# A hybrid encoder block: q and k of the second half of the heads are turned by VectorE and through memory instead of by TensorE, and some scalings and casts go to ScalarE

## The chip, the cores and the metric

The kernel runs on one core of one Trainium2 chip. The metric is the device time of one execution in microseconds; of several executions the median counts. Five engines work side by side: PE (TensorE, the matmuls), DVE (VectorE), ACT (ScalarE), POOL (GpSimd) and SP (SyncE, which only starts transfers). Each carries out its own list of instructions in a fixed order and waits on semaphores for the others. PEld is the loading of PE's stationary operand.

## The reference

One layer of an encoder over 512 tokens of width 1024 in float32:

```python
x = x + 0.5 * swiglu_1(rmsnorm(x))
h = rmsnorm(x)
xr, gr, q, k, v, ga, gb = split(h @ w_in)
xc = centred_dwconv(xr)                                   # width 4
y_lru = (rglru_forward(xc) + rglru_backward(xc)) * gelu(gr)
q = rmsnorm_per_head(q) * q_norm * 64 ** -0.5             # 16 heads of 64
k = rmsnorm_per_head(k) * k_norm
y_att = neighbourhood_attention(q, k, v, rel_pos_bias)    # grid of 8 rows x 64 columns, window 8 x 16
y = sigmoid(ga) * y_lru + sigmoid(gb) * y_att
x = x + y @ w_out
x = x + 0.5 * swiglu_2(rmsnorm(x))
```

## The kernel before, in words

All operands stay in SBUF as tiles of 128 partitions; feature-major tiles hold 128 features by 512 tokens. A float32 product is made of three matmuls: both factors are split into a high part (h) in a reduced format and the rest (l), and h·h, h·l and l·h are added in PSUM. For a weight, `load_w` fetches 128x1024 numbers as `wraw` on SP's queue, ScalarE writes `wh` (L138, or VectorE's cast L140 where `act` is false) and VectorE writes `wl` as the difference (L141). There are four buffers of `wh` and of `wl`, so the split of a chunk's weights waits for the last matmul of the chunk four before it. `feat_chunk` makes one output tile from eight such pieces: 24 matmuls of 128x512 (L165 to L167).

The program is, in order: the first FFN; the projections `wxr` with the convolution; six groups `wqkv` that make q, k and v token-major, for the two halves of the heads (hf 0 and 1, eight heads each); the merge gates (`gates`, 24 chunks of `wg3`: first the gelu gate of the recurrent branch, w = 0, then the two sigmoid gates as tanh); `wout`; the second FFN. Beside them run "lanes", Python generators that `weave` advances by the rates of `RATE` after each chunk or half chunk: the recurrence ("lru"), V through memory ("v"), and the attention ("att" and "tail").

The attention lane of a half is `heads`. It first scales q and k by the root mean square per head (L983). Then it goes through four tiles, fi = 0 to 3, of two heads each. `start(fi)` turns the token-major q and k into feature-major ones: eight transposes on PE into two PSUM tiles (L992, L994), from which ScalarE writes `qh` and `kh` (L998, L1001) and VectorE `ql` and `kl` (L1000, L1003), with the norm's gains `gq8` and `gk` multiplied in. The tile's scores are 24 matmuls (L1024; in the second half together, in the first twelve and twelve), the first of which reads `kl`. VectorE adds the bias and takes the maximum (L1044), ScalarE the exp with its sum (L1051), VectorE the reciprocal (L1053) and the product with 1/sum (L1056). `ship` turns the probabilities with VectorE's 32x32 transposes (L1065, L1066), stores them to memory (`pd`, SP's queue, L1068) and fetches them back regrouped (`PT`, four transfers on GpSimd's queue, L1072). `apply` multiplies them with V on PE (L1087) and ScalarE takes the result out of PSUM (`att`, L1097).

A merge gate's chunk ends in VectorE's product with 1/rms (L1150, `pair`), which also frees the PSUM tile; ScalarE applies gelu or tanh to two chunks at once (L1154), and VectorE multiplies by the branch (`A`, L1164, L1167, L1173, L1174).

The final order of each engine's list is made by a scheduler from the order in the program, priorities and its own estimate of times. `tc.high_priority()` moves an instruction forward, `after(a, b)` puts it behind another, and `hold` puts it behind the matmul that was emitted last. The kernel's own table `RATE` and these marks are thus what decides where the attention's steps stand among the chunks. `big_t` hands out one of 42 equal buffers (`NBIG`), `pair_t` one of four double ones.

Of the kernel before, what the change touches and what calls it, by code (L numbers as in the profile page):

```python
# [77 lines left out]
RATE = {  # L78
    "xr": {"att": 0.0, "lru": 2.75},
    "t0": {"att": 0.0, "lru": 3.25},  # L80
    "t1": {"att": 0.75, "tail": 0.75, "lru": 2},
    "g": {"att": 0.7, "tail": 0.7, "lru": 1.5, "v": 0.5},
}


# [1 line left out]
def block_kernel(ctx: ExitStack, tc, a, out):  # L87
# [156 lines left out]
    def hold(i):  # L244

        after(i, mark["mm"])
        return i
# [389 lines left out]
        end(t1, o)  # L637


    lanes = {"att": [], "tail": [], "lru": [], "v": []}  # L640
    due = {"att": 0.0, "tail": 0.0, "lru": 0.0, "v": 0.0}

    def weave(rate):
        for ln, n in rate.items():
# [138 lines left out]
    def lru():  # L783
# [52 lines left out]
        def use(f, d):  # L836
            r, ix = got[f, d]
            hold(nc.vector.tensor_tensor(ix, ix, xc[f], ALU.mult))
            th = big_t(n="th")
# [72 lines left out]
    def qk_raw(w, hf, st):  # L912
        raws = []
        for ps in tok_group(w, hf):
            t = big_t(n="qk")
            with tc.high_priority():
                copy = nc.scalar.activation(t, ps, AF.Copy)
            raws.append(t)
        for j, t in enumerate(raws):
            sq = big_t(n="sq")  # L920
# [46 lines left out]
            if g == 0:  # L967
                after(ld, mark["xr"])

    def heads(hf, raws, st):  # L970

        rq = tiny.tile([P, 2, NCB, 8], F32, tag="rq", name=nm("rq"))
        for w in range(2):
# [3 lines left out]
        hold(nc.scalar.activation(rq, rq, AF.Sqrt))  # L977
        nc.vector.reciprocal(rq, rq)
        yield
        for w in range(2):  # L980
            for j in range(NCB):
                t = raws[w][j].rearrange("p (h d) -> p h d", d=HD)
                hold(nc.vector.tensor_tensor(t, t, rq[:, w, j, :].unsqueeze(2).to_broadcast([P, 8, HD]), ALU.mult))  # L983
            yield
        qk, rss, soft, PTs = {}, {}, {}, {}


        def start(fi):
            fs = slice(fi * P, (fi + 1) * P)
            pq, pk = aux_t(), aux_t()  # L990
            for j in range(NCB):
                hold(nc.tensor.transpose(pq[:, j * P : (j + 1) * P], raws[0][j][:, fs], ident))  # L992
            for j in range(NCB):
                hold(nc.tensor.transpose(perm(pk)[:, j], raws[1][j][:, fs], ident))  # L994
# [3 lines left out]
            nc.scalar.activation(rev(qh), fwd(pq), AF.Copy, scale=gq8)  # L998
            with tc.high_priority():
                nc.vector.scalar_tensor_tensor(rev(ql), fwd(pq), gq8, rev(qh.bitcast(F32)), ALU.mult, ALU.subtract)  # L1000
            nc.scalar.activation(kh, pk, AF.Copy, scale=gk)  # L1001
            with tc.high_priority():
                mark["kl"] = nc.vector.scalar_tensor_tensor(kl, pk, gk, kh.bitcast(F32), ALU.mult, ALU.subtract)  # L1003
            grid = lambda t: t.rearrange("p (r c) -> p r c", r=ROWS)
            qk[fi] = qh, ql, grid(kh), grid(kl)

        def scores(fi, n2s):
# [22 lines left out]
            for n2, hp in [(n2, hp) for n2 in n2s for hp in range(2)]:  # L1030
# [22 lines left out]
                nc.vector.reciprocal(rs[:, hp, n2 * 2 : n2 * 2 + 2], rs[:, hp, n2 * 2 : n2 * 2 + 2])  # L1053
                for i, pt in enumerate(parts):
                    n = n2 * 2 + i
                    nc.vector.tensor_scalar(pt, pt, rs[:, hp, n : n + 1], None, ALU.mult)  # L1056
# [79 lines left out]
    for hf in range(2):  # L1136
        st = tiny.tile([P, 2, NCB, 8], F32, tag="st", name=nm("st"))
        raws = [qk_raw(0, hf, st), qk_raw(1, hf, st)]
        v_get(hf)
        lanes["att"].append(heads(hf, raws, st))  # L1140
        phase[0] = "t1" if hf == 0 else "g"


    def gates(w, fs, fn, scale=1.0):
        q = [pair_t() for _ in range((len(fs) + 1) // 2)]
        for i, f in enumerate(fs):
            ps = acc_t()
            feat_chunk(a["wg3"][w * KT + f], KT, xh, xl, ps, 0, KT, f % 2 == 0, RATE[phase[0]])
            with tc.high_priority():
                nc.vector.tensor_tensor(q[i // 2][:, i % 2], ps, rb, ALU.mult)  # L1150
            weave(RATE[phase[0]])
        for i, t in enumerate(q):
            n = min(2, len(fs) - 2 * i)
            nc.scalar.activation(t[:, :n], t[:, :n], fn, scale=scale)  # L1154
        return [(f, q[i // 2][:, i % 2]) for i, f in enumerate(fs)]
# [133 lines left out]
```

## Time and profile before

| | |
|---|---|
| median of 3 executions | 1088.83 us (1087.8 to 1089.4) |
| the profiled execution | 1086.2 us |
| its span, first to last instruction | 1084.4 us |
| matmuls of the span | 5121 |
| instructions of VectorE, ScalarE, GpSimd | 1222, 866, 340 |
| HBM read and written | 162.06 MB, 26.74 MB |

Rows of the profile read: start and length in us, engine, line of the kernel, operation, tiles written and read, shapes, count, and in brackets the idle time of that engine before it with the instruction that ended it. Rows of groups carry the number of instructions, their busy time and the mean of one in ns, then the idle time ahead of them. Rows of the chain of work that ended last carry start, length and group. In rows of DMA issues the last number is the median time from issue to landing. PE's matmuls overlap, so their durations in a timeline are longer than the time from one to the next.

### The profile page before, as it was taken

How to read it: one execution, taken by the hardware profiler on the slowest of the kernel's cores; microseconds unless marked ns; L12 is line 12 of the kernel's file. 1: busy time of each engine (PE TensorE's matmuls, PEld its weight loads, DVE VectorE, ACT ScalarE, POOL GpSimd, SP SyncE). 2: the span in 40 equal slices, each digit the busy share in tenths (PEclk: the TensorE clock that was granted, in tenths of full speed). 3: DMA queues.
4: the chain of work that ended last, by engine and by line, in shares of the span. 5: the costliest groups of instructions: out<-in, count | busy, mean ns of one | idle time of the engine just before them, and what ended most of it. 6: DMA issues, size and time to landing. Idle time of an engine off the chain costs nothing.

```text
span 1084.4 us, 14405 instructions
## 1 busy us (share of the span) xinstructions
PE 1076.1 (99%) x5121; PEld 883.1 (81%) x5121; DVE 770.8 (71%) x1222; ACT 562.1 (52%) x866; POOL 199.6 (18%) x340
## 2 busy tenths in 40 slices
PE   9999999999999999999999999999999999999998
PEld 7878888888888778788887888888888888888887
DVE  7798788774327876999868996759677787765322
ACT  7755554553215768877454642346455555544320
POOL 0101012432000441330345232000000001342000
PEclk9999999999999999999999999999999999999999
DMA  9878675975324675573787567564476777676222
GB/s 356 183 231 224 192 174 143 242 257 156 98 83 146 183 239 156 164 215 95 226 245 222 175 215 231 164 233 162 95 193 181 192 205 165 179 249 195 95 73 78
DMA packets 67464, 198.18 MB, mean 183 GB/s; under 512 B 11072, under 2 KB 12864, under 8 KB 67392
## 3 DMA queue, kind: packets, MB, share of 16 engines
q1 hardware_dynamic: 46736, 136.66, 37.6%
q0 software_dynamic: 20512, 60.34, 24.9%
q8 instruction: 40, 0.66, 0.3%
q14 instruction: 32, 0.26, 0.1%
q10 hardware_dynamic: 144, 0.26, 0.1%
HBM read 162.06 MB, written 26.74 MB: 174 GB/s over the span
## 4 chain that ended last, share of the span: by engine, by line
PE 95%; DVE 3%; issue 1%; DMA 1%; ACT 1%; SPq 0%; DVEq 0%; ACTq 0%
PE acc L315 19%; PE aux L315 14%; PE acc L165 10%; PE acc L166 10%; PE acc L167 10%; PE acc L905 4%; PE acc L906 4%; PE acc L907 4%; PE aux L166 4%; PE aux L167 4%; PE aux L165 4%; PE aux L1087 1%; PE aux L816 1%; PE aux L1024 1%; DVE wl L141 1%; PE aux L472 1%
## 5 line engine op out<-in xcount | busy, mean ns | idle before, releaser
L141 DVE TENSOR_TENSOR wl<-wraw,wh 128x1024 fp32r<-128x1024 f32 (+2 forms) x147 | 168.9, 1150 | 152.4 <-ACT wh L138 151.9
L138 ACT ACTIVATE wh<-wraw 128x1024 fp32r<-128x1024 f32 (+2 forms) x135 | 134.7, 999 | 214.9 <-PE acc L166 155.5
L141 DVE TENSOR_TENSOR wl<-pair,wh 128x1024 fp32r<-128x1024 f32 x80 | 97.5, 1222 | 43.7 <-ACT wh L138 43.5
L138 ACT ACTIVATE wh<-pair 128x1024 fp32r<-128x1024 f32 x80 | 84.7, 1062 | 77.5 <-PE aux L315 48.3
L165 PE MATMUL acc<-xh,wh 128*128 128x512 f32 x288 | 113.9, 396 | 0.0
L167 PE MATMUL acc<-xh,wl 128*128 128x512 f32 x288 | 112.5, 391 | 0.0
L166 PE MATMUL acc<-xl,wh 128*128 128x512 f32 x288 | 112.5, 391 | 0.0
L315 PE MATMUL aux<-wh,s 128*128 128x512 f32 x320 | 98.4, 389 | 0.2 <-ACT wh L138 0.2
L315 PE MATMUL acc<-wh,s 128*128 128x512 f32 x320 | 98.5, 389 | 0.0
L905 PE MATMUL acc<-wh,xh 128*128 128x512 f32 x192 | 75.7, 394 | 0.0
L906 PE MATMUL acc<-wh,xl 128*128 128x512 f32 x192 | 74.8, 389 | 0.0
L907 PE MATMUL acc<-wl,xh 128*128 128x512 f32 x192 | 74.7, 389 | 0.0
L315 PEld LDWEIGHTS aux<-wh,s 128*128 128x128 f32 x320 | 60.0, 188 | 13.0 <-ACT wh L138 0.6
L315 PEld LDWEIGHTS acc<-wh,s 128*128 128x128 f32 x320 | 60.1, 188 | 12.4
L166 PE MATMUL aux<-hl,wh 128*128 128x512 f32 (+1 forms) x179 | 69.3, 387 | 0.0
L167 PE MATMUL aux<-hh,wl 128*128 128x512 f32 (+1 forms) x179 | 69.3, 387 | 0.0
L165 PE MATMUL aux<-hh,wh 128*128 128x512 f32 (+1 forms) x179 | 69.0, 387 | 0.0
L167 PE MATMUL acc<-hh,wl 128*128 128x512 f32 (+1 forms) x176 | 68.1, 387 | 0.0
L166 PE MATMUL acc<-hl,wh 128*128 128x512 f32 (+1 forms) x176 | 68.1, 387 | 0.0
L165 PE MATMUL acc<-hh,wh 128*128 128x512 f32 (+1 forms) x176 | 68.0, 387 | 0.0
L165 PEld LDWEIGHTS acc<-xh,wh 128*128 128x128 f32 x288 | 54.1, 188 | 13.0 <-issue 2.3
L167 PEld LDWEIGHTS acc<-xh,wl 128*128 128x128 f32 x288 | 54.1, 188 | 11.5 <-issue 0.4
(230 smaller groups left out, 2416.5 us busy)
## 6 DMA issues: line engine op xcount, KB each, us to landing
wraw<-wqkv SPq DMA_DIRECT2D x24, 512.0 KB, 4.5
wraw<-wg SPq DMA_DIRECT2D x24, 512.0 KB, 7.5
wraw<-w1d SPq DMA_DIRECT2D x22, 512.0 KB, 4.2
wraw<-w2d SPq DMA_DIRECT2D x22, 512.0 KB, 3.3
PT<-w1s SPq DMA_DIRECT2D x20, 512.0 KB, 6.2
hT<-hd POOLq DMA_DIRECT2D x80, 128.0 KB, 4.2
PT<-w2s SPq DMA_DIRECT2D x20, 512.0 KB, 3.9
hd<-ht SPq DMA_DIRECT2D x32, 256.0 KB, 5.9
```

The source lines that it names most:

```text
L138: mark["H"] = nc.scalar.activation(H, raw, AF.Copy)
L141: return nc.vector.tensor_tensor(L, raw, H.bitcast(F32), ALU.subtract)
L165: nc.tensor.matmul(ps, wh, xh, start=first, stop=False, skip_group_check=skip)
L166: nc.tensor.matmul(ps, wh, xl, start=False, stop=False, skip_group_check=skip)
L167: mark["mm"] = nc.tensor.matmul(ps, wl, xh, start=False, stop=last, skip_group_check=skip)
L315: mark["mm"] = nc.tensor.matmul(pss[tb], x_[:, s], w_[:, c], start=first and k == 0 and x_ is xh_ and w_ is H, stop=k == 3 and w_ is L, sk ...
L472: nc.tensor.matmul(pre[tb], xh[k][:, s], H, start=k == 0, stop=False)
L816: prev, mm = mm, nc.tensor.matmul(ps[d][b], W[w][o, c], X[x][o], start=x == 1, stop=w + x == 0)
L905: nc.tensor.matmul(pss[j], xh[kk][:, tj], H[:, s], start=kk == 0, stop=False)
L906: nc.tensor.matmul(pss[j], xl[kk][:, tj], H[:, s], start=False, stop=False)
L907: mark["mm"] = nc.tensor.matmul(pss[j], xh[kk][:, tj], L[:, s], start=False, stop=kk == KT - 1)
L1024: mm = hold(nc.tensor.matmul(ps[hp][:, cs], q_[o, n * P : (n + 1) * P], keys(k_[o]), start=k_ is kl, stop=q_ is ql))
```

## The change

For the second half, hf = 1, `heads` is cut in two. A new lane, "prep", runs `norm_qk`: it scales q and k as before, turns each 128 tokens of them by 32x32 blocks on VectorE (L991), stores the four results (512 KB each) to memory as `qd` on SP's queue, and then fetches tile 0. `fetch(fi)` brings one tile's q and k back regrouped by four transfers on GpSimd's queue (L1010; each 32 partitions by 16 runs of 64 numbers) into the one buffer `xqk`; that of fi + 1 is emitted at the end of `start(fi)`. `start` of the second half has no transposes and reads `xqk` instead of PSUM. The gain of k is multiplied into that of q, so that `kh` and `kl` are a plain copy and difference; the copies to `qh` and `kh` are now held behind the matmul emitted last. The first half keeps its transposes (now L1027, L1029).

Besides, the products with 1/sum go from VectorE to ScalarE in both halves (L1098), and all casts of the merge gates' weights go to ScalarE, where before every second one was VectorE's. To make room, `NBIG` is 40, squares use the `pt` buffers and three `th` tiles those of `xqk` and `PT`. The multiply that ends a gate chunk is L1197 in the new file, `ql` and `kl` are L1040 and L1043, the maxima L1086, the score matmuls L1066, the A products L1211, `pt`'s transposes L1107 and L1108.

```diff
 RATE = {
...
-    "t1": {"att": 0.75, "tail": 0.75, "lru": 2},
-    "g": {"att": 0.7, "tail": 0.7, "lru": 1.5, "v": 0.5},
+    "t1": {"att": 0.75, "tail": 0.75, "lru": 2, "prep": 1.0},
+    "g": {"att": 0.7, "tail": 0.7, "lru": 1.5, "v": 0.5, "prep": 1.0},
...
-    NBIG = 42
+    NBIG = 40
...
-    gk = small[:, C_KN : C_KN + 1]
+    nc.vector.tensor_tensor(gq8, gq8, small[:, C_KN : C_KN + 1], ALU.mult)
...
-    def heads(hf, raws, st):
+    def norm_qk(raws, st, qd):
...
+        out = []
+        for j in range(NCB):
+            for w in range(2):
                 t = raws[w][j].rearrange("p (h d) -> p h d", d=HD)
                 hold(nc.vector.tensor_tensor(t, t, rq[:, w, j, :].unsqueeze(2).to_broadcast([P, 8, HD]), ALU.mult))
+            if qd is not None:
+                t2 = pair_t().rearrange("p a b -> p (a b)")
+                for w in range(2):
+                    nc.vector.transpose(
+                        t2.rearrange("p (c f w i) -> p w f c i", c=NCB, f=4, w=2)[:, w],
+                        raws[w][j].rearrange("p (f c i) -> p f c i", c=NCB, i=32))
+                while out:
+                    hold(nc.sync.dma_start(*out.pop()))
+                out.append((qd[j], t2))
+                yield
+            elif j % 2 == 1:
+                yield
+        if qd is not None:
+            hold(nc.sync.dma_start(*out.pop()))
             yield
+            fetch(qd, 0)
+
+    xs = {}
+
+    def fetch(qd, fi):
+        t = xs[fi] = big.tile([P, NCB * NCB, 2, 32], F32, tag="xqk", bufs=1, name=nm("xqk"))
+        for c in range(NCB):
+            hold(nc.gpsimd.dma_start(
+                t[c * 32 : (c + 1) * 32].rearrange("p g w i -> p g (w i)"),
+                qd.rearrange("j (a i) c f x -> c f i (j a) x", a=NCB)[c, fi]))
+
+    def heads(hf, raws, qd):
+
+        if hf == 1:
+            until("prep", lambda: False)
...
         def start(fi):
...
+            else:
+                x = xs.pop(fi).rearrange("p (j a) w i -> p w j a i", j=NCB)
+                xq, xk = x[:, 0], x[:, 1].rearrange("p j a (r c) -> p j a r c", r=2)
+                q_of = lambda t: rev(t).rearrange("p j (a i) -> p j a i", i=32)
+                k_of = lambda t: t.rearrange("p (a r j c) -> p j a r c", a=NCB, r=2, j=NCB)
             qh, ql, kh, kl = (big_t(F32R, n=n) for n in ("qh", "ql", "kh", "kl"))
-            nc.scalar.activation(rev(qh), fwd(pq), AF.Copy, scale=gq8)
+            hold(nc.scalar.activation(q_of(qh), xq, AF.Copy, scale=gq8))
...
-            nc.scalar.activation(kh, pk, AF.Copy, scale=gk)
+            hold(nc.scalar.activation(k_of(kh), xk, AF.Copy))
             with tc.high_priority():
-                mark["kl"] = nc.vector.scalar_tensor_tensor(kl, pk, gk, kh.bitcast(F32), ALU.mult, ALU.subtract)
+                mark["kl"] = nc.vector.tensor_tensor(k_of(kl), xk, k_of(kh.bitcast(F32)), ALU.subtract)
+            if hf == 1 and fi < 3:
+                fetch(qd, fi + 1)
...
-                    nc.vector.tensor_scalar(pt, pt, rs[:, hp, n : n + 1], None, ALU.mult)
+                    nc.scalar.activation(pt, pt, AF.Copy, scale=rs[:, hp, n : n + 1])
...
-            feat_chunk(a["wg3"][w * KT + f], KT, xh, xl, ps, 0, KT, f % 2 == 0, RATE[phase[0]])
+            feat_chunk(a["wg3"][w * KT + f], KT, xh, xl, ps, 0, KT, True, RATE[phase[0]])
```

The edit moves instructions by way of the scheduler. First TensorE's list of the kernel before, where the scores of the second half's tile 0 begin (acc is the PSUM tile of a gate chunk):

```order
L165 MATMUL acc_1060_5388<-xh_541_2740,wh_1062_5390 128x512
L994 MATMUL aux_1065_5408<-ident_82,qk_889_4560 128x8x16
L166 MATMUL acc_1060_5388<-xl_542_2741,wh_1062_5390 128x512
L167 MATMUL acc_1060_5388<-xh_541_2740,wl_1063_5391 128x512
L1024 MATMUL aux_1074_5459<-kl_1069_5420,qh_1066_5417 128x256
L1024 MATMUL aux_1073_5458<-kl_1069_5420,qh_1066_5417 128x256
L1024 MATMUL aux_1074_5459<-kh_1068_5419,qh_1066_5417 128x256
L1024 MATMUL aux_1073_5458<-kh_1068_5419,qh_1066_5417 128x256
```

The same place in the changed kernel:

```order
L167 MATMUL acc_1055_5338<-xh_539_2738,wl_1058_5341 128x512
L165 MATMUL acc_1055_5338<-xh_541_2740,wh_1057_5340 128x512
L166 MATMUL acc_1055_5338<-xl_542_2741,wh_1057_5340 128x512
L167 MATMUL acc_1055_5338<-xh_541_2740,wl_1058_5341 128x512
L1066 MATMUL aux_1066_5385<-kl_1062_5360,qh_1059_5357 128x256
L1066 MATMUL aux_1065_5384<-kl_1062_5360,qh_1059_5357 128x256
L1066 MATMUL aux_1066_5385<-kh_1061_5359,qh_1059_5357 128x256
L1066 MATMUL aux_1065_5384<-kh_1061_5359,qh_1059_5357 128x256
```

The transposes are gone from between the matmuls; the scores still follow directly on the last matmul of a chunk, which here is the sixth of the gelu gate.

VectorE's list of the kernel before, at `kl` of the same tile:

```order
L1000 SCALAR_TENSOR_TENSOR ql_1067_5418<-aux_1064_5407,gq8_2898,qh_1066_5417 128x4x128
L983 TENSOR_TENSOR qk_888_4558<-qk_888_4558,rq_1053_5315 128x512
L983 TENSOR_TENSOR qk_889_4560<-qk_889_4560,rq_1053_5315 128x512
L140 CAST wh_1156_5808<-wraw_1155_5807 128x1024
L1150 TENSOR_TENSOR pair_1044_5260<-acc_1060_5388,rstd_559_2947 128x512
L1003 SCALAR_TENSOR_TENSOR kl_1069_5420<-aux_1065_5408,small_78,kh_1068_5419 128x512
L141 TENSOR_TENSOR wl_1157_5809<-wraw_1155_5807,wh_1156_5808 128x1024
```

VectorE's list of the changed kernel at the same place, the twelve rows that end with `kl` and the transpose after it; the multiply (L1197) of the chunk whose matmuls stand in the rows of TensorE above, acc_1055, and one `wl` stand a few rows further ahead, with maxima between:

```order
L1086 ISA nmx_1037_5248 128x1
L1086 ISA so_1036_5247,nmx_1037_5248<-aux_1031_5223,bm_978_4954 128x192
L1086 ISA nmx_1037_5248 128x1
L1095 RECIPROCAL rs_1011_5126<-rs_1011_5126 128x2
L1211 TENSOR_TENSOR A_1045_5293<-pair_980_4962,th_631_3254 128x512
L1211 TENSOR_TENSOR A_1046_5295<-pair_980_4962,th_660_3384 128x512
L1211 TENSOR_TENSOR A_1047_5297<-pair_981_4963,th_693_3513 128x512
L1211 TENSOR_TENSOR A_1048_5299<-pair_981_4963,th_713_3593 128x512
L1095 RECIPROCAL rs_1011_5126<-rs_1011_5126 128x2
L1040 SCALAR_TENSOR_TENSOR ql_1060_5358<-xqk_1005_5087,gq8_2898,qh_1059_5357 128x4x128
L1043 TENSOR_TENSOR kl_1062_5360<-xqk_1005_5087,kh_1061_5359 128x4x8x16
L1108 STREAM_TRANSPOSE pt_1040_5275<-p_1033_5237 128x4x4x32
```

Between the multiply and `kl` there now stand the maxima of the first half's last scores and four A products.

VectorE's list at `kl` of the second half's tile 1, before:

```order
L1000 SCALAR_TENSOR_TENSOR ql_1098_5557<-aux_1095_5546,gq8_2898,qh_1097_5556 128x4x128
L1053 RECIPROCAL rs_1072_5457<-rs_1072_5457 128x2 x2
L1065 STREAM_TRANSPOSE pt_1089_5526<-p_1077_5486 128x3x4x32
L1003 SCALAR_TENSOR_TENSOR kl_1100_5559<-aux_1096_5547,small_78,kh_1099_5558 128x512
L1056 TENSOR_SCALAR p_1080_5489<-p_1080_5489,rs_1072_5457 128x256
L1150 TENSOR_TENSOR pair_1107_5578<-acc_1109_5580,rstd_559_2947 128x512
```

And in the changed kernel:

```order
L1197 TENSOR_TENSOR pair_1050_5302<-acc_1100_5530,rstd_559_2948 128x512
L141 TENSOR_TENSOR wl_1190_5937<-wraw_1188_5935,wh_1189_5936 128x1024
L1040 SCALAR_TENSOR_TENSOR ql_1088_5473<-xqk_1063_5365,gq8_2898,qh_1087_5472 128x4x128
L1043 TENSOR_TENSOR kl_1090_5475<-xqk_1063_5365,kh_1089_5474 128x4x8x16
L1197 TENSOR_TENSOR pair_1140_5697<-acc_1142_5699,rstd_559_2948 128x512
```

Here acc_1100 is the chunk in front of tile 1's scores on TensorE; its multiply and a `wl` now stand ahead of `ql` and `kl`. In the kernel before, the scores of tiles 1 to 3 stand in the middle of a chunk, whose multiply comes after `kl`.

GpSimd's list of the changed kernel around the fetch of the second half's tile 3:

```order
L969 DMA bm_1184_5900<-rpb 128x640
L1010 DMA xqk_1133_5678<-qd_4619 32x16x64
L1114 DMA PT_1125_5655<-pd_1124_5653 32x4x224 x4
L1114 DMA PT_1128_5665<-pd_1127_5663 32x4x224 x4
L1010 DMA xqk_1133_5678<-qd_4619 32x16x64 x3
```

One of the fetch's four transfers stands ahead of two groups of `PT` fetches, three behind them.

More of the change, by code (lines that the diff above doesn't have):

```diff
@@ L637, in ffn @@
         end(t1, o)
-    lanes = {"att": [], "tail": [], "lru": [], "v": []}
-    due = {"att": 0.0, "tail": 0.0, "lru": 0.0, "v": 0.0}
+    lanes = {"att": [], "tail": [], "lru": [], "v": [], "prep": []}
+    due = {"att": 0.0, "tail": 0.0, "lru": 0.0, "v": 0.0, "prep": 0.0}
     def weave(rate):
@@ L838, in use @@
             hold(nc.vector.tensor_tensor(ix, ix, xc[f], ALU.mult))
-            th = big_t(n="th")
+            if d == 1 and f < 3:
+                th = big.tile([P, T], F32, name=nm("th"), **(dict(tag="xqk", bufs=1) if f == 0 else dict(tag="PT", bufs=5)))
+            else:
+                th = big_t(n="th")
             act("tanh", nc.scalar.activation(th, r, AF.Tanh, scale=sp4[:, f * 2 + d : f * 2 + d + 1]))
@@ L919, in qk_raw @@
         for j, t in enumerate(raws):
-            sq = big_t(n="sq")
+            sq = big.tile([P, T], F32, tag="pt", bufs=2, name=nm("sq"))
             after(nc.scalar.activation(sq, t, AF.Square), copy)
@@ L979, in heads @@
         yield
-        for w in range(2):
-            for j in range(NCB):
+        out = []
+        for j in range(NCB):
+            for w in range(2):
                 t = raws[w][j].rearrange("p (h d) -> p h d", d=HD)
                 hold(nc.vector.tensor_tensor(t, t, rq[:, w, j, :].unsqueeze(2).to_broadcast([P, 8, HD]), ALU.mult))
-            yield
+            if qd is not None:
[10 more added lines that the diff above has]
+                yield
@@ L985, in heads @@
         qk, rss, soft, PTs = {}, {}, {}, {}
         def start(fi):
[L989 to L994, printed above, removed]
-            rev = lambda t: t.rearrange("p (j t) -> p j t", j=NCB)[:, :, ::-1]
-            fwd = lambda t: t.rearrange("p (j t) -> p j t", j=NCB)
+            rev = lambda t: t.rearrange("p (j t) -> p j t", j=NCB)[:, :, ::-1]
@@ new lines, in start @@
+            if hf == 0:
+                fs = slice(fi * P, (fi + 1) * P)
+                pq, pk = aux_t(), aux_t()
+                for j in range(NCB):
+                    hold(nc.tensor.transpose(pq[:, j * P : (j + 1) * P], raws[0][j][:, fs], ident))
+                for j in range(NCB):
+                    hold(nc.tensor.transpose(perm(pk)[:, j], raws[1][j][:, fs], ident))
+                xq, xk = pq.rearrange("p (j t) -> p j t", j=NCB), pk
+                q_of, k_of = rev, lambda t: t
+            else:
+                x = xs.pop(fi).rearrange("p (j a) w i -> p w j a i", j=NCB)
+                xq, xk = x[:, 0], x[:, 1].rearrange("p j a (r c) -> p j a r c", r=2)
+                q_of = lambda t: rev(t).rearrange("p j (a i) -> p j a i", i=32)
+                k_of = lambda t: t.rearrange("p (a r j c) -> p j a r c", a=NCB, r=2, j=NCB)
@@ L997, in start @@
             qh, ql, kh, kl = (big_t(F32R, n=n) for n in ("qh", "ql", "kh", "kl"))
-            nc.scalar.activation(rev(qh), fwd(pq), AF.Copy, scale=gq8)
+            hold(nc.scalar.activation(q_of(qh), xq, AF.Copy, scale=gq8))
             with tc.high_priority():
-                nc.vector.scalar_tensor_tensor(rev(ql), fwd(pq), gq8, rev(qh.bitcast(F32)), ALU.mult, ALU.subtract)
-            nc.scalar.activation(kh, pk, AF.Copy, scale=gk)
+                nc.vector.scalar_tensor_tensor(q_of(ql), xq, gq8, q_of(qh.bitcast(F32)), ALU.mult, ALU.subtract)
@@ L1138, in block_kernel @@
         raws = [qk_raw(0, hf, st), qk_raw(1, hf, st)]
+        if hf == 1:
+            qd = dram.tile([NCB, P, NCB, 4, 64], F32, name="qd")
+            lanes["prep"].append(norm_qk(raws, st, qd))
         v_get(hf)
-        lanes["att"].append(heads(hf, raws, st))
+        if hf == 0:
+            lanes["att"].append(norm_qk(raws, st, None))
+        lanes["att"].append(heads(hf, raws, qd if hf == 1 else None))
         phase[0] = "t1" if hf == 0 else "g"
```

## The prediction

> **What bounds the kernel now.** I read the page's busy times and its chain first, then what TensorE waited for, then the stretch that the change touches.
>
> ```profile
> PE 1076.1 (99%) x5121; PEld 883.1 (81%) x5121; DVE 770.8 (71%) x1222; ACT 562.1 (52%) x866; POOL 199.6 (18%) x340
> PE 95%; DVE 3%; issue 1%; DMA 1%; ACT 1%; SPq 0%; DVEq 0%; ACTq 0%
> PE aux L1024 <- DVE kl L1003: 1.8, 1, 1.8
> 500.00:560.00 60.00, 60.00 (x351) 48.55 (x350) 49.51 (x130) 28.62 (x71) 14.33 (x25) 1.00 0.63 197
> 560.00:620.00 60.00, 58.19 (x373) 46.93 (x372) 51.21 (x141) 34.06 (x72) 27.85 (x44) 1.00 0.73 207
> 620.00:660.00 40.00, 40.00 (x261) 33.34 (x260) 35.45 (x96) 16.72 (x44) 11.53 (x20) 1.00 0.65 209
> ```
>
> TensorE is busy 1076.1 of 1084.4 us. So only two things move the end: TensorE work that goes, and idle time of TensorE that comes or goes. In the stretch of the attention and merge gates (columns of the window rows: length, busy time and count for PE, PEld, DVE, ACT, POOL, then clock) PE is idle once, for 1.8 us, and VectorE is busy 51.2 of 60 us, ScalarE 34.1. VectorE work that leaves is worth nothing by itself.
>
> That one idle time is the key to this change. VectorE's timeline, then PE's, around it:
>
> ```profile
> 594.42 0.69 DVE L140 CAST wh<-wraw 128x1024 fp32r<-128x1024 f32 x1 [1.62 <-PE acc L166]
> 595.03 0.68 DVE L1150 TENSOR_TENSOR pair<-acc,rstd 128x512 f32<-128x512 f32 x1
> 595.63 0.74 DVE L1003 SCALAR_TENSOR_TENSOR kl<-aux,small,kh 128x512 fp32r<-128x512 f32 x1
> 596.29 1.22 DVE L141 TENSOR_TENSOR wl<-wraw,wh 128x1024 fp32r<-128x1024 f32 x1
> 594.22 0.40 PE L167 MATMUL acc<-xh,wl 128*128 128x512 f32 x1
> 596.43 0.40 PE L1024 MATMUL aux<-kl,qh 64*128 64x256 f32 x2 [1.81 <-DVE kl L1003]
> ```
>
> The score matmuls of the second half's first tile stand directly behind the last matmul of a merge-gate chunk. Their first operand, kl, stands on VectorE behind the cast and the multiply that wait for that same last matmul. So PE must stand while VectorE works off everything between "chunk done" and "kl done": 0.69 + 0.68 + 0.74, less the overlap of neighbours, is the 1.81. Nothing can hide such a wait: it is made by the two orders.
>
> **The change, part by part.**
>
> *What leaves TensorE.* 32 of the 64 transposes (L992, L994) go, those of the second half.
>
> ```profile
> L992 PE MATMUL aux<-ident,qk 128*128 128x128 f32 x32 | 5.7, 287 | 0.0
> L994 PE MATMUL aux<-ident,qk 128*128 128x128 f32 x32 | 5.4, 277 | 0.0
> 591.27 0.26 PE aux L994
> 591.53 1.24 PE aux L1087 x20
> ...
> 596.43 1.00 PE aux L1024 x12
> 597.43 0.76 PE acc L1024 x12
> 598.20 0.59 PE aux L992 x4
> 598.78 0.44 PE aux L994 x4
> 599.22 0.23 PE acc L165
> ```
>
> Back to back, eight cost 0.59 + 0.44 = 1.03 us on the chain; singly between other matmuls one costs 0.26. Of the 32, three groups of eight stand together (3.1 us) and one group is spread (8 x 0.26 = 2.1): 5.2 us; at 0.44 / 4 = 0.11 each the floor is 3.5. The old stall goes too, 1.8, since it belongs to an order that no longer exists. Saved: 7.0 us (5.3 to 7.0).
>
> *What leaves VectorE and comes to ScalarE.* 64 multiplies by 1/sum and 12 casts:
>
> ```profile
> L1056 DVE TENSOR_SCALAR p<-p,rs 128x192 f32<-128x192 f32 (+1 forms) x64 | 18.9, 334 | 0.3
> L140 DVE CAST wh<-wraw 128x1024 fp32r<-128x1024 f32 x12 | 8.3, 689 | 16.1 <-PE acc L166 15.2 <-PE acc L906 1.0
> L138 ACT ACTIVATE wh<-pair 128x1024 fp32r<-128x1024 f32 x80 | 84.7, 1062 | 77.5 <-PE aux L315 48.3
> 599.12 0.46 ACT L1051 ACTIVATE p<-so,nmx 128x192 f32<-128x192 f32 x1
> 599.58 0.50 ACT L1051 ACTIVATE p<-so,nmx 128x256 f32<-128x256 f32 x1
> ```
>
> ScalarE gets 64 at about 0.4 (an estimate: the exp on the same tiles takes 0.46 to 0.50 with a sum that the scaling doesn't have; less than 0.33, VectorE's price, would surprise me) and 12 x 1.06, together some 38 us in a stretch of 160 of which it was busy 28.6 + 34.1 + 16.7 = 79.4. By load it has room. The cover is gone only where ScalarE stands in the path to kl, and that is counted next.
>
> *The new place of kl.* In the changed order all four score groups of the second half stand right behind the last matmul of a gate chunk, and in all four that chunk's multiply (now L1197) stands ahead of kl (now L1043) on VectorE. One such stall of 1.81 becomes four. Each is priced by what stands between the two, with these durations beside those above:
>
> ```profile
> 594.25 0.69 ACT L1001 ACTIVATE kh<-aux,small 128x512 fp32r<-128x512 f32 x1 [3.43 <-PE aux L994]
> 594.84 0.59 ACT L1097 ACTIVATE att<-aux 128x512 f32<-128x512 f32 x1
> 595.45 1.28 ACT L1154 ACT_TABLE_LOAD   x1
> 596.74 1.06 ACT L1154 ACTIVATE pair<-pair 128x1024 f32<-128x1024 f32 x1
> 571.22 0.38 DVE L1044 CUSTOM_DVE_ANT_0 so<-aux,bm 128x256 f32<-128x256 f32 x1
> 573.78 0.67 DVE L1164 TENSOR_TENSOR A<-pair,th 128x512 f32<-128x512 f32 x1
> 570.63 0.66 DVE L1066 STREAM_TRANSPOSE pt<-p 128x512 f32<-128x512 f32 x1
> L1000 DVE SCALAR_TENSOR_TENSOR ql<-aux,gq,qh 128x512 fp32r<-128x512 f32 x8 | 6.0, 744 | 2.2 <-ACT qh L998 2.2
> ```
>
> Two paths lead to kl, VectorE's own queue and ScalarE's up to qh and kh; the longer counts.
> - Tile 0. VectorE: multiply 0.68, wl 1.22, four maxima at 0.38, four A products at 0.6 (0.67 less overlap), ql 0.74, kl 0.74 and two short reciprocals: 7.5. ScalarE: wh 1.06 (its buffer comes free with that chunk), gelu 1.06, table load 1.28, four exps 1.9, att 0.59, two scalings 0.8, qh and kh 1.4, then kl: 8.8. I take 8.7.
> - Tile 1. VectorE: 0.68, wl 1.22, ql, kl: 3.4. ScalarE: wh 1.06, table load 1.28, gelu 1.06, qh and kh 1.4, then kl 0.74: 5.5.
> - Tile 2. VectorE: 0.68, eight maxima 3.0, wl 1.22, two pt transposes 1.1, reciprocals 0.4, ql, kl: 7.9. ScalarE has the whole softmax of tile 1 in front of kh: wh 1.06, att 0.59, table load 1.28, eight exps at 0.48, six scalings at 0.4, qh and kh 1.4, then kl: 11.3 by durations; some of it is overlap of neighbours, so 11.0.
> - Tile 3. wh 1.06 and wl 1.22 behind it, ql, kl: 3.8.
>
> Sum 29.0; by VectorE alone, with ScalarE at nothing, 7.5 + 3.4 + 7.9 + 3.4 = 22.2. Below that it cannot go: these instructions stand in that order.
>
> *The way through memory.* Eight VectorE transposes of q and k (L991) at 0.66 come to 5.3 us. They cost nothing: VectorE has 10.5 us free in 500 to 560, and the first half's 32 scalings (32 x 0.33 = 10.7) leave it before the same place. Four stores of 512 KB join SP's queue; weights are loaded chunks ahead there and the DMA engines stand at 0.63 to 0.73 (the windows' last column but one), so they cost nothing either. The 16 fetches stand on GpSimd's queue, in order, among fetches of PT that wait for pd to land:
>
> ```profile
> pd<-pt SPq DMA_DIRECT2D x16, 448.0 KB, 5.3
> va<-vd POOLq DMA_DIRECT2D x16, 64.0 KB, 3.8
> 569.09 1.60 POOL L954 DMA_DIRECT2D va<-vd  x2
> 613.02 4.41 POOL L1072 DMA_DIRECT2D PT<-pd  x8 [9.80 <-DMA pd<-pt]
> ```
>
> The nearest row to a fetch (L1010: runs of 64 numbers, 256 bytes, 32 partitions of 16) is va<-vd, runs of the same length but half as many: 0.8 to issue, 3.8 to land. The fetch of tile 3 is the tight one. Three of its four stand behind the PT fetches of tile 1's softmax, whose last transposes follow kl of tile 2: transposes 1.1, pd 0.3 + 5.3, four PT issues 2.2, three issues 2.3, landing 3.8: 15.0 us after kl of tile 2. Needed, by the chain's rows above: 24 score matmuls 1.8, 32 PV matmuls at 1.24 / 20 2.0, two chunks of 24 matmuls at 0.23 11.0, wh 1.06: 15.9 us after. It arrives 0.9 us early, so I add nothing; if it lands slower, that goes straight onto the wait of tile 3. Tile 1's fetch has 3 us to spare, the others more.
>
> In the first half nothing is added: no chunk's multiply stands between kl and the scores there, and the order on PE up to that place is unchanged; the scalings on ScalarE lie beside chunks, whose next operands are cast three chunks ahead.
>
> **Clock.** A PE that stands for 9 to 11 us may come back slower. The rows that bear on it:
>
> ```profile
> 1.06 3.36 PE L132 MATMUL aux<-ones 128*128 128x128 f32 x14 [1.06 <-DVE pol L741]
> 596.00:598.00 2.00, 1.57 (x24) 1.53 (x24) 2.00 (x5) 1.97 (x3) 0.00 (x0) 1.00 0.09 38
> ```
>
> At the start of the kernel the same form of matmul as the transposes came every 3.36 / 14 = 0.24 us instead of 0.11; after the stall of 1.81 us nothing was slower, and the granted clock column stayed 1.00. If such a slow start of 3.4 to 3.8 us follows each stall over 5 us, it loses (1 - 0.11 / 0.24) x 3.6 = 2.0 us three times: 6 us. I count it at nothing, since the only stall inside the kernel that can be seen shows nothing, and keep the 6 for the range. The Trainium skill speaks against that choice (TensorE: Matmul & The Clock Gate, "Part 1: The HAM clock gate"): PE's clock halves after an idle window of about 3.4 us and comes back after as long a busy one. By that page the loss would be 1.7 us for each of the three long stalls, about 5 us more than my sum; the trace has no idle time that long after its start, so no row here shows it.
>
> **Sum.** 1086.2 us is the profiled execution's own time (span 1084.4 and 1.8 around it); the median of the runs is 1088.8, 2.6 above, and I put the difference on the median. +29.0 for the four waits, -7.0 for transposes and the old wait: +22.0, so 1110.8 us.
>
> **Rivals.**
> - *The forecast*: four waits, 1110.8. Its own range runs from VectorE alone (+15.2: 1104.0) to full durations without overlap and a late tile 3. 0.50.
> - *Slow return after long waits*: the same waits, and PE restarts at half pace: 1110.8 + 6.0 = 1116.8. For it: 0.24 against 0.11 at the start. Against: 1.81 us left no trace. 0.20.
> - *Late fetches*: the runs of 256 bytes land at twice the 3.8 of va<-vd (there are twice as many); tile 3 waits 2.9 more (3.8 less the 0.9 to spare), tile 1 0.8: 1114.5. For it: the fetches share a queue that waited 9.80 us for pd in the row above. Against: 0.9 to 3 us to spare, and a DMA share of 0.65. The Trainium skill holds that transfers under 512 bytes miss line rate by a read-modify-write (DMA: Bandwidth & Descriptors, "Specifications"); va<-vd at 3.8 for 64 KB beside pd<-pt at 5.3 for 448 KB agrees. 0.12.
> - *Shorter waits*: only multiply, ql and kl (2.2) count on tiles 1 and 3, and half of VectorE's queue on 0 and 2, were it to run faster on a standing PE: 2 x 2.2 + 3.8 + 4.0 = 12.2, +5.2: 1094.0. It contradicts the durations above. 0.06.
> - *No wait worth the name: faster.* If each tile waited only as the one of the trace does, for multiply and kl, 1.4 us, the four would come to 5.6 and the change to -1.4; if kl were done before PE arrives, to -7.0: 1081.8. It decides at 7.0 / 4 = 1.75 us a tile. For it: PE waited on one tile of four before, though VectorE was as full. Against: in the order of before only that one kl stands behind the multiply of the chunk that its scores follow. 0.09 faster, 0.03 about the same.
>
> **How the numbers follow.** Forecast, slow return and late fetches hold 0.82 of the chance and lie between 1104 and 1119 with their own spread; the range 1102 to 1119 takes these in and leaves out the shorter and the vanishing waits, 0.18. Slower by over 0.2% (2.2 us, about what a measurement of this kernel can tell from none): 0.88; within it 0.03; faster 0.09.
>
> **What would show it.** In the changed kernel's profile PE should wait for kl L1043 four times, about 8.7, 5.5, 11.0 and 3.8 us, in the rows of what PE waited for; PE's busy time should fall by some 5 us; each wait should begin at the last matmul of a gate chunk, with L1197 the first VectorE instruction in it, and qh or kh (ScalarE) the releaser of kl. Idle time ended by xqk on ScalarE would speak for late fetches; a PEclk under 9, or 24 score matmuls taking over 1.8 us after a wait, for the slow return. Wrong it is if L1197 runs before the PE's chunk ends there, or if PE's waits for kl come to less than 7 us in all.

## The result, and the profile after

| | before | after |
|---|---|---|
| median | 1088.63 us (4 runs, 1087.8 to 1089.4) | 1118.16 us (4 runs, 1117.71 to 1119.81) |
| ratio, 95% interval | | 1.0272 [1.0260, 1.0285] |
| span of the profiled execution | 1084.4 us | 1116.8 us |
| granted TensorE clock, mean | 1.000 | 0.986 |

The kernel became 2.7% slower. The page of the changed kernel, its busy times and clock, and below them what TensorE waited for (us in total, times, longest):

```profile
PE 1079.6 (97%) x5089; PEld 887.2 (79%) x5089; DVE 753.6 (67%) x1155; ACT 597.2 (53%) x942; POOL 207.4 (19%) x356
PEclk9999999999999999999998889999999999999999
PE aux L1066 <- DVE kl L1043: 28.0, 4, 10.7
PE aux L1129 <- DVE ql L1040: 2.0, 1, 2.0
PE acc L908 <- ACT qk L920: 1.0, 1, 1.0
```

Four waits for kl, 28.0 us, stand where one of 1.8 stood. Two more, 3.0 us, are new in the first half. And PE's busy time rose by 3.5 us although 32 transposes left it: its granted clock fell below 9 tenths in just the slices of the waits (the row PEclk, 40 slices of the span), so the matmuls there took longer. TensorE's timeline has the four waits, in the order of the tiles:

```profile
591.31 0.58 PE L1066 MATMUL aux<-kl,qh 64*128 64x256 f32 x2 [8.38 <-DVE kl L1043]
613.89 0.58 PE L1066 MATMUL aux<-kl,qh 64*128 64x256 f32 x2 [5.38 <-DVE kl L1043]
644.15 0.58 PE L1066 MATMUL aux<-kl,qh 64*128 64x256 f32 x2 [10.68 <-DVE kl L1043]
665.66 0.58 PE L1066 MATMUL aux<-kl,qh 64*128 64x256 f32 x2 [3.54 <-DVE kl L1043]
```

The chain of work that ended last goes through the first of them (start, length, what):

```profile
582.71 0.24 PE acc L167
582.97 0.70 DVE pair L1197
583.71 1.05 ACT pair L1201
584.77 1.28 ACT L1093
586.07 1.04 ACT p L1093 x4
...
589.26 0.62 ACT qh L1038
589.90 0.55 DVE ql L1040
590.57 0.70 DVE kl L1043
591.31 1.65 PE aux L1066 x10
...
595.39 0.43 PE acc L167
...
596.62 0.23 PE acc L167
```

It is the forecast's path but for two steps of about the same length: last matmul of the chunk, its multiply (the forecast had wh, which ran beside it), gelu, table load, exps, qh, ql (the forecast had kh, also beside it), kl, scores. The last two rows show what the forecast left out of its sum: the chunk matmuls behind the wait take 0.43 us each for a while, then 0.23 again. TensorE alone in stretches of that time (length, busy time and count, granted clock, DMA share, GB/s), for tile 0:

```profile
586.00:587.00 1.00, 0.00 (x0) 0.60 0.95 229
595.00:596.00 1.00, 1.00 (x3) 0.50 0.63 177
596.00:597.00 1.00, 1.00 (x5) 0.78 0.51 131
597.00:598.00 1.00, 1.00 (x6) 1.00 0.79 177
```

And for the ends of the slow stretches of tiles 1 to 3:

```profile
616.00:617.00 1.00, 1.00 (x9) 0.54 0.79 197
...
646.00:647.00 1.00, 1.00 (x12) 0.50 0.85 284
647.00:648.00 1.00, 1.00 (x14) 0.68 0.82 300
...
670.00:671.00 1.00, 1.00 (x14) 0.50 0.00 0
671.00:672.00 1.00, 1.00 (x13) 0.73 0.00 0
```

The clock falls to half some 3.3 us into the wait of tile 0 and comes back only when PE has worked again for 5.1 us (591.31 to about 596.4). On tiles 1 to 3 it takes 3.0, 3.5 and 5.9 us: together 17.5 us of work at half pace, 8.8 us lost if all of it ran at half speed. So the span's +32.4 is 28.0 for kl, less 1.8 for the old wait, +3.0 in the first half, +8.8 for the clock; the rest, -5.6, falls to the transposes. A run of the same work without slow stretches (below, with the fetch on SP) puts the transposes at 4.4 and, by PE's busy time, 1079.6 - 1071.7 = 7.9 on the clock. So the two sizes are known to about 1 us.

### The profile page after: what moved, and what is told of

It is laid out like the page before. It is cut to its first block, busy times and chain, and to the rows that moved or that the text cites. A ratio compares the mean times of both kernels' runs of the same rounds, so it can differ in the third digit from the quotient of the medians.

```text
span 1116.8 us, 14398 instructions
## 1 busy us (share of the span) xinstructions
PE 1079.6 (97%) x5089; PEld 887.2 (79%) x5089; DVE 753.6 (67%) x1155; ACT 597.2 (53%) x942; POOL 207.4 (19%) x356
## 4 chain that ended last, share of the span: by engine, by line
PE 88%; DVE 5%; ACT 3%; DMA 2%; issue 1%; POOL 0%; SPq 0%; ACTq 0%; DVEq 0%
PE acc L315 19%; PE aux L315 14%; PE acc L165 10%; PE acc L166 10%; PE acc L167 10%; PE aux L166 4%; PE aux L167 4%; PE aux L165 4%; PE acc L908 3%; PE acc L909 3%; PE acc L910 3%; PE aux L1129 2%; DVE wl L141 1%; PE aux L816 1%; ACT p L1093 1%
## 5 line engine op out<-in xcount | busy, mean ns | idle before, releaser
L138 ACT ACTIVATE wh<-wraw 128x1024 fp32r<-128x1024 f32 (+2 forms) x147 | 147.3, 1003 | 272.0 <-PE acc L166 201.8
L165 PEld LDWEIGHTS acc<-xh,wh 128*128 128x128 f32 x288 | 54.4, 189 | 13.7 <-issue 2.7
```

Source lines behind the costliest of these rows:

```text
L138: mark["H"] = nc.scalar.activation(H, raw, AF.Copy)
L165: nc.tensor.matmul(ps, wh, xh, start=first, stop=False, skip_group_check=skip)
```

## The experiments

**The path through memory alone.** Which part makes the waits? The changed kernel with both moves to ScalarE taken back.

```diff
-                    nc.scalar.activation(pt, pt, AF.Copy, scale=rs[:, hp, n : n + 1])
+                    nc.vector.tensor_scalar(pt, pt, rs[:, hp, n : n + 1], None, ALU.mult)
...
-... xh, xl, ps, 0, KT, True, RATE[phase[0]])
+... xh, xl, ps, 0, KT, f % 2 == 0, RATE[phase[0]])
```

> The way through memory alone: products with 1/sum and every second cast back on VectorE. Theory (the four waits come from where kl stands behind a chunk's multiply): the order still has a chunk's multiply ahead of kl on all four tiles, so TensorE waits for kl four times again, 25 to 29 us in all (tile 0 longer, about 9.7, since four products with 1/sum and two transposes come between; tile 2 shorter on ScalarE), with the slow restart behind the long ones: 1112 to 1119 us. Rival (the work moved to ScalarE makes the waits): waits under 10 us in all, 1090 us or less.

Measured: 1112.44 us, ratio to before 1.0225 [1.021, 1.0241], four waits for kl:

```profile
PE aux L1066 <- DVE kl L1043: 25.1, 4, 10.7
```

They are 10.68, 4.34, 6.55 and 3.54 us: tile 0 longer and tile 2 shorter than in the changed kernel, as the two paths of the forecast have it. No wait is left in the first half. So the waits come with the way through memory, and not with the load on ScalarE; which part of it makes them, the load or the order, is asked below.

**The moves to ScalarE alone**, the reverse, on the kernel before.

```diff
-                    nc.vector.tensor_scalar(pt, pt, rs[:, hp, n : n + 1], None, ALU.mult)
+                    nc.scalar.activation(pt, pt, AF.Copy, scale=rs[:, hp, n : n + 1])
...
-... xh, xl, ps, 0, KT, f % 2 == 0, RATE[phase[0]])
+... xh, xl, ps, 0, KT, True, RATE[phase[0]])
```

> The kernel before with only the products with 1/sum and all gate casts on ScalarE. Theory: no chunk's multiply stands ahead of kl on any of the four tiles, so the old wait of 1.8 us goes and no new one comes: 1086.5 to 1088.5 us. Rival (ScalarE, 38 us more work, is the bound in this stretch): waits on ScalarE's tiles, 1095 us or more. The rival of the changed kernel's 3 us of new waits in the first half: if they come from the scalings there, they show here too; if from the buffers or the transposes on VectorE, they don't.

Measured: 1086.81 us, ratio 0.9992 [0.9983, 1.0002]. The wait for kl is gone, and one as long has come in the first half:

```profile
PE acc L905 <- ACT qk L917: 2.1, 1, 2.1
```

ScalarE takes q and k out of PSUM there (L917), and in its queue these copies stood behind exps, two pairs of scalings (0.84 us a pair), qh, a wh and kh. What one part gains the other gives back. That ScalarE's 38 us more are no bound was right; that the scalings cost the first half nothing was not.

**The multiply behind kl.** One mark for the scheduler on the changed kernel.

```diff
+            if hf == 1:
+                mark["kl1"] = mark["kl"]
...
-                nc.vector.tensor_tensor(q[i // 2][:, i % 2], ps, rb, ALU.mult)
+                m = nc.vector.tensor_tensor(q[i // 2][:, i % 2], ps, rb, ALU.mult)
+            if "kl1" in mark:
+                after(m, mark["kl1"])
```

> The changed kernel with one order mark more: in the second half the multiply of a gate chunk stands behind the kl emitted last, so kl, and all in front of it, is done during the chunk. Nothing is taken out. Theory: the waits for kl fall from 28.0 us to 0 to 6, the clock stays up, and the saving of the transposes remains: 1083 to 1090 us. Rival (the fetches through memory are late, and the order only hides it): the waits stay above 20 us, then with ScalarE's qh waiting for xqk: 1110 us or more.

Measured: 1109.32 us, 1.0195 [1.018, 1.021]: a miss. The waits for kl fell from 28.0 only to 14.7, and 4.1 came elsewhere: a chunk's first matmul waited for its accumulator, whose old scores were still to be read by maxima behind a late wl. The trace says why; ScalarE's timeline, then VectorE's, at tile 0 of this run:

```profile
581.29 1.06 ACT L138 ACTIVATE wh<-wraw 128x1024 fp32r<-128x1024 f32 x1 [4.38 <-PE acc L166]
582.36 1.28 ACT L1095 ACT_TABLE_LOAD   x1
582.38 1.23 DVE L141 TENSOR_TENSOR wl<-wraw,wh 128x1024 fp32r<-128x1024 f32 x1 [4.21 <-ACT wh L138]
583.52 0.42 DVE L1088 CUSTOM_DVE_ANT_0 so<-aux,bm 128x256 f32<-128x256 f32 x1
```

Both engines idle over 4 us during the chunk, then start with wh and wl, whose buffers come free with the chunk's last matmuls; maxima, whose scores were made at 567.5 to 568.5, and exps are queued behind. The multiply is one of three instructions that wait for the chunk's end, and moving it alone leaves the other two ahead of kl.

**The weights' split behind kl too.**

```diff
+            if "kl2" in mark:
+                after(mark["H"], mark["kl2"])
```

In `split`, with kl2 set to a tile's kl where its scores are emitted; the mark of the run before stays.

> As the run before with kl first, and the split of the weights (wh, wl) of chunks that are emitted after a tile's scores stands behind that tile's kl too. What the last run left open: with the multiply moved, 18.8 us of waits stayed, and on tile 0 both engines idled 4 us, then started with wh and wl, whose buffer comes free at the same chunk end, with the maxima and exps queued behind. Theory (whatever waits for the chunk's end and stands ahead of kl makes the wait, wh and wl as well as the multiply): waits for kl of 3 to 7 us in all, 1087 to 1094 us. Rival (VectorE and ScalarE have too much to do between the scores of one tile and kl of the next, whatever the order): waits stay at 14 us or more, 1105 us or more.

Measured: 1098.53 us, 1.0098 [1.0079, 1.0117]. Waits for kl 8.1 us, above the 3 to 7; 5.1 of these are on tile 1, and there the reason is a new one. ScalarE, then GpSimd:

```profile
600.88 0.72 ACT L1040 ACTIVATE qh<-xqk,gq 128x512 fp32r<-128x512 f32 x1 [5.18 <-DMA PT<-pd]
594.84 2.19 POOL L1120 DMA_DIRECT2D PT<-pd  x4 [4.59 <-PE aux L1135]
597.02 0.67 POOL L1012 DMA_DIRECT2D xqk<-qd  x1
```

The fourth transfer of xqk was issued at 597.02, behind a PT fetch that had waited for TensorE, and qh began 3.9 us later. The profile puts the end of qh's wait to PT, which qh doesn't read; that it was xqk, on the same queue, I take from qh's operands. With the order put right, the late fetch of the forecast's rival is then the next limit. In the changed kernel itself no instruction waited for xqk.

**Idle matmuls in the waits.** Is the fallen clock the cause of the slow stretches? Matmuls that nothing needs keep TensorE busy; the numbers are those of tiles 0 to 3.

```diff
+FILL = (60, 36, 0, 0)
...
+            if hf == 1:
+                for _ in range(FILL[fi]):
+                    hold(nc.tensor.matmul(pss[0][0][:, :P], ident, ident, start=True, stop=True))
```

> The changed kernel with 60 idle matmuls of 128x128 in front of tile 0's scores and 36 in front of tile 1's, into the PSUM tile that the scores then overwrite: they need nothing that is late, so TensorE works through most of the two waits (60 x 0.12 = 7.2 of 8.4, 36 x 0.12 = 4.3 of 5.4). Theory (the clock falls after an idle time of several us): kl comes no earlier, but the granted clock stays at 1.00 behind tiles 0 and 1 and the loss there, about 2.6 and 1.6 us, goes: 1113 to 1115 us. Rival (the slow matmuls behind a wait have another cause, such as the engines working off their queues): still slow, 1118 us or a little more.

Measured: 1120.99 us, 1.0298 [1.0280, 1.0315], outside what either side expected: 60 of them took 13.56 us, 0.23 each and not 0.12 (I had the price of the transposes; the trace counts each of these matmuls as two instructions, a transpose as one), so they overran the waits by about 5 and 3 us. The clock stayed at 1.00 behind both tiles. Again with `FILL = (34, 20, 0, 0)`:

> The idle matmuls once more, fewer: 34 in front of tile 0's scores and 20 in front of tile 1's. In the run with 60 and 36 they took longer than the waits (no wait was left on these tiles), at about 0.21 us each. Now 34 x 0.215 = 7.3 of 8.4 us and 20 x 0.215 = 4.3 of 5.4. Theory (the clock falls because TensorE stands): granted clock 1.00 behind tiles 0 and 1, the loss there of 2.6 and 1.5 us gone, nothing else changed: 1113.5 to 1115 us. Rival (another cause): 1118 us.

Measured: 1113.75 us, 1.0234 [1.0218, 1.0251]: 4.4 us below the changed kernel, where 2.6 + 1.5 = 4.1 was forecast. kl came no earlier: it started at 590.21 where it had been 590.57, and TensorE's last wait before the scores is short (the 34 idle matmuls, the scores, and a stretch behind them with the clock at 1.00, the last column but two):

```profile
582.40 7.75 PE L1060 MATMUL aux<-ident 128*128 128x128 f32 x68
591.04 0.40 PE L1071 MATMUL aux<-kl,qh 64*128 64x256 f32 x2 [0.89 <-DVE kl L1045]
592.00:594.00 2.00, 2.00 (x20) 1.65 (x17) 1.91 (x13) 1.51 (x7) 0.79 (x2) 1.00 0.75 214
```

Keeping TensorE busy with nothing made the kernel faster, so the idle time makes the clock fall, and the fall is a cost of its own.

**Only the casts** of the gates on ScalarE, on the kernel before.

```diff
-... xh, xl, ps, 0, KT, f % 2 == 0, RATE[phase[0]])
+... xh, xl, ps, 0, KT, True, RATE[phase[0]])
```

> The kernel before with all gate casts on ScalarE and nothing else. Theory: kl of the second half's tile 0 then stands ahead of the chunk's multiply, so the 1.8 us wait goes; the first half is as before, so the 2.1 us wait that came with the scalings on ScalarE doesn't appear: 1086.0 to 1086.8 us on a before of 1088. Rival (the casts themselves put load where it tells): no gain, 1088 us or more.

Measured: 1084.56 us, 0.9966 [0.9953, 0.9978], 5 rounds: faster than both kernels. TensorE's timeline at tile 0 has the scores right behind the chunk:

```profile
594.20 0.39 PE L167 MATMUL acc<-xh,wl 128*128 128x512 f32 x1
594.51 0.39 PE L1024 MATMUL aux<-kl,qh 64*128 64x256 f32 x2
```

The span fell from 1084.4 to 1082.6, the 1.8 us. The medians differ by 4 us, and the clock suggests why. Of the 74 executions of the kernel before that were timed beside the experiments, 17 had a mean granted clock of 1.000 (median 1087.3 us), 14 of 0.999 (1087.8) and 43 of 0.998 (1089.1). Of the six here five had 1.000 and one 0.999. One stretch of 3.4 us at half clock makes a mean of 0.998 and costs up to 1.7 us. So in most of its executions the kernel before seems to lose such a stretch, which the wait of 1.8 us may bring; the profiled one, with 1.000, is not of these. No trace of another was kept, so the place of the stretch is not shown.

**The fetch on SP's queue**, the changed kernel else untouched.

```diff
-            hold(nc.gpsimd.dma_start(
+            hold(nc.sync.dma_start(
```

> The changed kernel with the fetches of q and k on SP's queue instead of GpSimd's, nothing else by hand. The scheduler then puts kl elsewhere: on tile 0 ahead of the chunk's multiply, on tiles 1 and 3 directly behind it, on tile 2 behind it and one wl. Theory (the order of kl behind what waits for the chunk's end makes the waits): tile 0 up to 2 us, tiles 1 and 3 about 1.4 each, tile 2 about 3: 5 to 8 us of waits, little or no fall of the clock, 1088 to 1094 us. Rival (the work between two tiles' scores is too much whatever the order): 20 us of waits or more, 1108 us or more. Rival (transfers of 256-byte runs land late on any queue): qh waits for xqk on ScalarE by several us.

Measured: 1089.02 us, 1.0010 [0.9998, 1.0021]: 29 us below the changed kernel.

```profile
PE 1071.7 (99%) x5089; PEld 880.1 (81%) x5089; DVE 752.4 (69%) x1155; ACT 600.3 (55%) x944; POOL 197.6 (18%) x340
PEclk9999999999999999999999999999999999999999
PE aux L1066 <- DVE kl L1043: 5.7, 3, 2.8
PE aux L1129 <- DVE ql L1040: 2.4, 1, 2.4
PE acc L908 <- ACT qk L920: 1.0, 1, 1.0
```

The work between the scores is the same; kl stands elsewhere, and the waits are 5.7 us. With a mean clock of 1.000 in this execution, TensorE's busy time shows what the transposes were worth: 1076.1 - 1071.7 = 4.4 us. This run changes queue and order together. That the order does it, and not the queue, rests on the runs with marks: they kept GpSimd's queue and the work, and the waits for kl went from 28.0 to 14.7 and to 8.1 us. That the scheduler put kl late because it expects GpSimd's fetch late is argued, not shown.

**All of it put together**: the two marks, the fetch on SP, the first half's scalings back on VectorE. Then the same with all scalings on VectorE. To the three edits above comes, in the first:

```diff
-                    nc.scalar.activation(pt, pt, AF.Copy, scale=rs[:, hp, n : n + 1])
+                    if hf == 0:
+                        nc.vector.tensor_scalar(pt, pt, rs[:, hp, n : n + 1], None, ALU.mult)
+                    else:
+                        nc.scalar.activation(pt, pt, AF.Copy, scale=rs[:, hp, n : n + 1])
```

> What the runs so far point to, put together: kl ahead of the multiply and of the weights' split (as in the run with kl before wl), the fetch on SP's queue, so that tile 1's qh doesn't wait 5 us for a fetch behind PT, and the products with 1/sum of the first half back on VectorE, so that the first half has no new wait. Theory: waits of 0 to 4 us in all, the transposes' 5.2 and the old wait's 1.8 are kept: 1081 to 1087 us, faster than before. Rival (too much work between the scores): 1095 us or more.

> As the run before, with the products with 1/sum on VectorE in both halves. Theory: kl hangs on ScalarE's path more than on VectorE's (8.8 against 7.5 us on tile 0, 11.0 against 7.9 on tile 2), so this is as fast or up to 3 us faster: 1080 to 1087 us. Rival (VectorE is the fuller engine there, 51 of 60 us, and the products on it delay kl): 2 to 5 us slower than the run before.

Measured: 1085.74 us, 0.9979 [0.9963, 0.9995], and 1086.34, 0.9983 [0.9970, 0.9997]. Both faster than before, and no different from each other within their intervals: where the scalings are doesn't tell once kl is early. TensorE no longer waits for kl in either. The first waits for wh and wl instead, and behind these waits the clock is at half for 3.4 us (the second waits 1.6 and 0.5 us for them, and 1.7 and 2.1 for fetches of V and PT):

```profile
PE acc L167 <- ACT wh L138: 1.9, 1, 1.9
PE acc L169 <- DVE wl L143: 0.9, 1, 0.9
```

**Two tries at removing these as well**: without the mark on the split; and without either mark, with qh and kh at high priority. The second has, for `kh` likewise:

```diff
-            hold(nc.scalar.activation(q_of(qh), xq, AF.Copy, scale=gq8))
+            with tc.high_priority() if hf == 1 else nullcontext():
+                hold(nc.scalar.activation(q_of(qh), xq, AF.Copy, scale=gq8))
```

> The changed kernel with the fetches on SP's queue, the first half's products with 1/sum back on VectorE, and the multiply of a chunk behind the kl emitted last, but no mark on the weights' split (the run with all early waited 1.9 us for wh and 0.9 for wl). Theory: no wait for kl, for ql or for wh: the run with only the fetch on SP had 5.7 + 2.4 + 1.0 us of them at 1089.0: 1080 to 1084 us. Rival (kl early pushes the multiply back, and the accumulators come free late): a wait on a chunk's first matmul, 1085 us or more.

> The same without the mark on the multiply, but with qh and kh of the second half at high priority: the scheduler's own order then has kl ahead of the multiply on tiles 0 and 2 and directly behind it on 1 and 3. Theory: two waits of 1.4 to 1.5 us, as in the run with the fetch on SP, and nothing in the first half: 1089.0 - 3.4 - 2.8 = 1082.8 us (1081 to 1085). Rival (the first half's waits don't come from the scalings there): 2 to 3 us stay there, 1086 us.

Measured: 1089.72 us, 1.0010 [1.0001, 1.0019], and 1090.01, 1.0011 [0.9997, 1.0024]: two misses. The first half's waits are gone in both, as expected of the scalings, but kl is waited for again, 6.2 and 4.5 us, and in the second a PT fetch for 2.9. Behind the waits the clock is at half for 3.4 us in the first and 10.2 in the second. ScalarE's timeline in the first of them, at tile 2:

```profile
631.30 0.71 ACT L1038 ACTIVATE qh<-xqk,gq 128x512 fp32r<-128x512 f32 x1
635.02 1.06 ACT L138 ACTIVATE wh<-wraw 128x1024 fp32r<-128x1024 f32 x1 [3.01 <-PE acc L166]
635.98 0.61 ACT L1041 ACTIVATE kh<-xqk 128x512 fp32r<-128x512 f32 x1
```

kh, ready to go at 632, stands behind a wh that waits for the chunk's end: the same fault on another engine. Four of the five runs with the fetches on SP's queue, all but the one that moves only them, have ScalarE wait 7.5 to 10.8 us for weights loaded by the same queue; in the second of the two runs:

```profile
ACT wh L138 <- DMA wraw<-wg: 10.8, 2, 5.5
```

In the kernel before and in the changed one there was no such wait. Whether the fetches delay these loads is not shown: the delayed loads of this run were issued right behind stores of pd, which waited for VectorE. None of the runs that keep the way through memory beats the one with the casts alone.

## Why the prediction was right, point by point

- *kl behind the chunk's end, four times.* Right in place, cause and size: forecast 8.7, 5.5, 11.0 and 3.8, measured 8.38, 5.38, 10.68 and 3.54. The durations of the old trace, added along the order of the new kernel, gave 29.0 for 28.0. Where I named the multiply as the reason, the runs add the split of the weights, which the sums held but the words did not: wh and wl wait for the end of the same chunk, and with only the multiply moved 18.8 us of waits stayed.
- *Slow return, counted at nothing.* This step failed: I put it at nothing, and it cost 7.9 to 8.8 us. Of the two rows at hand I took the stall of 1.81 us, behind which nothing was slow in the one execution that was profiled; the nearer one was the kernel's start, 0.24 against 0.11. The rival with its 2.0 us for each long wait had the right size (8.8 in four; it had expected three), and the range held the result because this rival set its upper end. The idle matmuls show the cause.
- *The number, and luck in it.* The sum put +22.0 on the span, which rose by 32.4: 10.4 short, about 8.8 for the clock and 3.0 for the first half, less 1.0 for the waits. The median missed by only 7.4 (1118.16 for 1110.8), because I added the 2.6 us by which the median of before lay above its profiled execution. The changed kernel's median lies 0.4 below its own, so these 3 us are luck.
- *PE's busy time.* It should have fallen by some 5 us and rose by 3.5, which is the clock again.
- *Transposes.* 5.2 forecast, 4.4 by PE's busy time in the run with the clock up; the old wait of 1.8 went, as forecast.
- *First half at nothing.* Wrong by 3.0 us. I looked for a chunk's multiply ahead of kl there, and not for what stands behind the scalings in ScalarE's queue: the copies of q and k out of PSUM (1.0 here, 2.1 with the moves alone). The other 2.0, PV waiting for a PSUM tile that ql still reads, appears (0.5 to 2.4 us) in every run that has the first half's scalings on ScalarE together with the path, and in none of the seven that lack one of the two; why it takes both is not shown.
- *Late fetches.* Not in this kernel. The landing, 3.0 us at the median and 6.9 at most, was mostly shorter than the 3.8 that I took from va<-vd; but once kl was early qh of tile 1 waited 5.2 us, by my reading for one.
- *ScalarE's load.* Right that 38 us more have room by load, and that what tells is its place in the path.

## What to carry to other kernels

Look in the new order for what stands, on each engine, between an instruction that waits for the bound engine's last result and the one that the bound engine needs next; add the durations from the old trace, along the longest path over the engines: with up to 0.3 us taken off for overlap it gave each wait here within 0.4 us. An edit that takes a little off the bound engine can move such a place through the scheduler, and then costs several times what it saves. Price an idle time of the bound engine above its length when the clock depends on its being busy. And compare the profiled execution with the median before you read from it what leaves no trace: here it was one of the quicker ones, with the clock up.

## What the runs showed of the hardware

- TensorE's clock fell to 0.50 not only behind long waits. Behind one of 2.06 us (the run with the split behind kl) it was at half at once:

```profile
641.00:642.00 1.00, 0.00 (x0) 1.00 0.77 205
642.00:643.00 1.00, 0.96 (x8) 0.50 0.47 139
```

  Of three waits of 2.78 us (in the runs with the fetch on SP) one was followed by half clock and two were not; the one of 1.81 us in the profiled execution of before was not; one of 1.69 us (all scalings on VectorE) was, 1.6 us after TensorE had resumed. In the changed kernel the clock is at half for 10.2, 3.4, 10.2 and 6.8 us, and in the other traces for 3.4, 6.8, 10.2 or 13.7: multiples of about 3.41. The Trainium skill (TensorE: Matmul & The Clock Gate, "Part 1: The HAM clock gate") has a free-running window of about 3.4 us, and the half pace and these multiples agree with that; the falls behind 2.06 and 1.69 us of idle time don't agree with a whole idle window, and the measurement decides.
- A matmul of 128x128 float32 with an identity took 0.23 us from one to the next, a transpose by the same identity 0.11. The trace has two instructions for the matmul (68 for the 34 above) and one for the transpose, so at clock 1.00 each instruction takes 0.11; the 0.24 of the kernel's start is per instruction, and thus half pace, though the granted clock reads 1.00 there too.
- The same 16 fetches of 256-byte runs were 8192 packets under 512 B more on SP's queue than on GpSimd's, and 7680 packets more in all; the page's lines of the changed kernel and of the run with the fetch on SP:

```profile
DMA packets 68809, 202.38 MB, mean 181 GB/s; under 512 B 11392, under 2 KB 13184, under 8 KB 68736
```

```profile
DMA packets 76489, 202.38 MB, mean 186 GB/s; under 512 B 19584, under 2 KB 21376, under 8 KB 76416
```

  16 fetches of 32 x 16 runs are 8192: on SP each run is a packet of its own. The 512 packets between 2 and 8 KB that are gone are as many as 16 x 32 partitions: on GpSimd's queue the 16 runs of a partition, 4 KB, went as one.
